# Modulation vectors of a diffusion block: TensorE matmuls with the weights as moving operand, in four column quarters, where VectorE made multiply-and-sum passes

## The chip, the core and the metric

The kernel runs on one core of a Trainium2 chip. The metric is device microseconds of one execution, as a median over runs. The core's engines are TensorE (PE, with its weight loads shown apart as PEld), VectorE (DVE), ScalarE (ACT) and GpSimd (POOL); SyncE (SP) issues the DMA transfers. Each engine works through its own instructions in program order and waits on semaphores for the others.

## What is computed

The program is a first block (a gated delta rule mixer and a convolutional GLU, both modulated) followed by a second block of two layers. Only the first one's modulation is touched:

```python
s_lat = jax.nn.silu(c)[:, None, :]            # [1, 1, 1024]
s_ctx = jax.nn.silu(c_ctx)[None, None, :]
mod_l = jnp.split(s_lat @ w_mod[i] + b_mod[i], 6, axis=-1)   # w_mod [1024, 6144]
mod_c = jnp.split(s_ctx @ w_mod[i] + b_mod[i], 6, axis=-1)
h_lat = modulate(rms_norm(x_lat, norm1_g[i]), mod_l[0], mod_l[1])
h_ctx = modulate(rms_norm(x_ctx, norm1_g[i]), mod_c[0], mod_c[1])
y_ctx, y_lat = gdn_mixer(h_ctx, h_lat, ...)
x_lat = x_lat + mod_l[2] * y_lat
h_lat = modulate(rms_norm(x_lat, norm2_g[i]), mod_l[3], mod_l[4])
x_lat = x_lat + mod_l[5] * conv_glu(h_lat, ...)
```

The sequence has 512 positions, the context 256, the model 1024 features. `mod_l` is a vector of 6144 values, and of `mod_c` only the first 2048 are used. The first 2048 of both are needed before anything can enter the mixer's projections; the other 4096 of `mod_l` only after the mixer.

## The kernel before

Features lie on partitions, positions on columns. A modulation vector is kept by feature: `modl` is [128, 48] (column j holds features 128j to 128j+127), `modc` is [128, 16]. Weights come from DRAM in blocks [128, 1024] (512 KB) through `wraw` (L136), a ring of three buffers. For most products ACT makes a rounded high part (L110), DVE or POOL the low part (L119), and TensorE takes three matmuls for each k tile (L157 to L159).

Stages of the first block, in the order of the program text:

- **mod**: `Modulation.__init__` makes silu of `c` and `c_ctx` by feature, and spreads both as rows over all partitions (`rowl`, `rowc`: 16 diagonal tiles on DVE, L1292, 16 matmuls with a matrix of ones, L1293, 4 copies on ACT, L1294). `by_tensor` makes columns 9 to 15 of both vectors: 7 blocks of w_mod stationary, two moving columns, 56 matmuls (L1316). `column(j, 1024)` makes columns 0 to 8: a load of 128 rows of w_mod's transpose, then for each of the two vectors one pass of DVE that multiplies by the silu row and sums (L1305), 18 passes.
- **h**: the norm of x and of the context (L247 to L256), and `modulated`: for each of 8 k tiles x * r (L1338, on POOL here), a high part on ACT (L1349), the modulated value (L1350) and the low part (L119) on DVE.
- **gat, prep0 to prep7**: the mixer's projections head by head, and small inverses (`inv`).
- **scan0 to scan3**: the recurrence by pairs of heads; scan 0, then scan 1, then 2 and 3 together. Lines L1653 to L1744.
- **fill**: work that the second block and the gates need, listed in `others` as units with a cost each: 8 gates (5.1), the norm of the memory (5), for each of two layers 8 blocks of keys (2.6) and 4 of values (5.1). Units are written into the program until their summed cost passes 32 ahead of the scans, and 4.6 more for each step of a scan. `mod.column(j, 512, ...)` for the other 32 columns of `modl` stands inside the gates, keys and values: two loads of 256 KB (`fill_C`) and two passes of DVE (L1305) each, 64 in all.
- **gout**: the mixer's output product, which needs all scans; `modl` is next used from there on.

The recorder that builds the program puts each engine's instructions into an order of its own, by dependencies, with the scans' steps at a higher priority than the fills; so the place of a fill is known from the built program.

Of the kernel before, what the change touches and what calls it, by code (L numbers as in the profile page):

```python
# [27 lines left out]
class Prog:  # L28
    """The program's pools and the parts that its stages share. Tiles of one tag are handed out in the order
    of the program, so what is to run ahead has a tag of its own."""  # L30
# [21 lines left out]
    def tiles(self, name, **kw):  # L52
        """a pool whose tiles wait for the users of their own bytes alone"""
        return self.tc.tile_pool(name=name, bufs=1, reuse_waits="tile", **kw)

    @contextmanager
    def pool(self, name, keep=False, **kw):
        """tiles of a stage; with keep, of several stages (tile(..., keep=True))"""
# [13 lines left out]
    def xt(self, dtype=F32R):  # L72
        """tiles of the products' operand, of all stages"""
# [6 lines left out]
    def banks(self, **bufs):  # L80
        """cuts PSUM's 8 banks in tags; within another, those that it leaves"""
# [24 lines left out]
    # exact split of a float32 value in two parts of 12 significant bits  # L106
# [14 lines left out]
    def split(self, src, tag, bufs, scale=None, n=512, le="v", keep=False, pool=None):  # L121
        """(hi, lo) of src, or of src * scale (scale: one value per partition)"""
# [38 lines left out]
    def gemm_block(self, ps, w, X, C, c0, kt, n=512, k0=0, first=True, last=True):  # L161
        """ps[128, n] += sum_k w[:, k, c0:c0+128]^T X[k]"""
# [7 lines left out]
    def strip(self, name, b, X, n=512):  # L170
        """block b of 128 output features: [128, n] in PSUM"""
# [4 lines left out]
    def rows_gemm(self, name, b0, X, pst):  # L176
        """products by position: pst[t] = X[:, tile t]^T w, 512 columns, in blocks of two k tiles"""
# [41 lines left out]
    def rsqrt(self, src, n, y, m, t, parts=1):  # L219
        """y = (src / n + EPS) ** -0.5, m = src / n + EPS; one Newton step on exp(-log(m) / 2); in parts of the  # L220
        columns where the next step waits for it"""
# [20 lines left out]
    def square_add(self, acc, x, last=False, scale=1.0):  # L242
        """acc + (scale * x) ** 2, per partition"""
# [9 lines left out]
    def rstd_rows(self, acc, n, width=512):  # L253
        """1 / rms by position, on all partitions"""
# [11 lines left out]
    def sigmoid(self, z, a):  # L266
        """a = 1 / (1 + exp(-z))"""
        nc = self.nc
        nc.vector.scalar_tensor_tensor(a, z, -1.0, z, ALU.mult, ALU.min)     # -|z|
        nc.scalar.activation(a, a, AF.Exp)  # L270
        nc.scalar.activation(a, a, AF.Ln, bias=self.one)
        nc.vector.scalar_tensor_tensor(a, z, 0.0, a, ALU.min, ALU.subtract)  # log of the sigmoid
# [4 lines left out]
def blocks(w, cols, C, kt=None):  # L277
    """[K, N] -> [nb, 128, kt * C]: block b holds columns cols[b*C:(b+1)*C], K split in kt tiles"""
# [28 lines left out]
def rope_tables():  # L307
    """cos, sin of 16 frequencies, 8 times; sin with the signs of the keys' products"""
# [1779 lines left out]
```

## Time and profile before

| | us |
|---|---|
| median of three runs (lowest to highest) | 3739.19 (3737.09 to 3744.71) |
| span of the profiled execution | 3736.5 |
| PE busy, share of the span | 3565.1, 95% |
| DVE busy, share of the span | 2461.0, 66% |
| ACT busy, share of the span | 1780.5, 48% |
| POOL busy, share of the span | 1273.6, 34% |

The profile is of one execution, on the kernel's one core. The table of windows shows the busy time of each engine in a stretch, the number of instructions in brackets, and the granted clock of TensorE as a share of 2.4 GHz (0.50 is the lower level, 1.2 GHz). Matmuls are pipelined: the record of one is longer than the distance to the next, so a busy PE can still be waiting inside its pipeline. "Idle before" is the time an engine stood still ahead of a group, with what ended it.

### The profile page before, as it was taken

How to read it: one execution, taken by the hardware profiler on the slowest of the kernel's cores; microseconds unless marked ns; L12 is line 12 of the kernel's file. 1: busy time of each engine (PE TensorE's matmuls, PEld its weight loads, DVE VectorE, ACT ScalarE, POOL GpSimd, SP SyncE). 2: the span in 40 equal slices, each digit the busy share in tenths (PEclk: the TensorE clock that was granted, in tenths of full speed). 3: DMA queues.
4: the chain of work that ended last, by engine and by line, in shares of the span. 5: the costliest groups of instructions: out<-in, count | busy, mean ns of one | idle time of the engine just before them, and what ended most of it. 6: DMA issues, size and time to landing. Idle time of an engine off the chain costs nothing. (4 is left out here: it accounts for less than half of the span.)

```text
span 3736.5 us, 51792 instructions
## 1 busy us (share of the span) xinstructions
PE 3565.1 (95%) x19280; PEld 2872.1 (77%) x19280; DVE 2461.0 (66%) x3770; ACT 1780.5 (48%) x3214; POOL 1273.6 (34%) x1173
## 2 busy tenths in 40 slices
PE   7998899899999998999999999999998999999998
PEld 5887788778888776687777888876676877778886
DVE  8887685655535788875556665369888755556643
ACT  3766454344434354565544443245456555444431
POOL 4476774322211555332121221125544311212212
PEclk7999899999999898999999999998899999999999
DMA  5346675433343111222243333421112322533332
GB/s 171 104 108 179 205 236 168 138 132 97 98 123 109 46 57 51 84 80 87 85 152 102 118 97 99 128 89 49 44 52 80 102 73 90 161 113 96 96 101 91
DMA packets 228955, 401.04 MB, mean 107 GB/s; under 512 B 77280, under 2 KB 118496, under 8 KB 228704
## 3 DMA queue, kind: packets, MB, share of 16 engines
q1 hardware_dynamic: 228704, 397.74, 34.7%
q8 instruction: 152, 2.49, 0.3%
q14 instruction: 99, 0.81, 0.1%
HBM read 347.58 MB, written 47.97 MB: 106 GB/s over the span
## 5 line engine op out<-in xcount | busy, mean ns | idle before, releaser
L159 PE MATMUL ffn_psg<-xo_X,ffn_wl 128*128 128x512 f32 x704 | 274.7, 390 | 0.0
L158 PE MATMUL ffn_psg<-xo_X,ffn_wh 128*128 128x512 f32 x704 | 273.9, 389 | 0.0
L157 PE MATMUL ffn_psg<-xo_X,ffn_wh 128*128 128x512 f32 x704 | 273.9, 389 | 0.0
L119 DVE TENSOR_TENSOR ffn_wl<-ffn_wr,ffn_wh 128x1024 fp32r<-128x1024 f32 x88 | 153.5, 1745 | 19.7 <-ACT ffn_wh L110 19.7
L719 DVE TENSOR_TENSOR ffn_z<-ffn_psg,xo_ry 128x512 f32<-128x512 f32 x88 | 60.7, 691 | 142.9 <-PE ffn_psg L159 142.6
L157 PEld LDWEIGHTS ffn_psg<-xo_X,ffn_wh 128*128 128x128 f32 x704 | 132.1, 188 | 27.9 <-issue 0.5
L159 PEld LDWEIGHTS ffn_psg<-xo_X,ffn_wl 128*128 128x128 f32 x704 | 132.1, 188 | 27.8 <-issue 0.5
L158 PEld LDWEIGHTS ffn_psg<-xo_X,ffn_wh 128*128 128x128 f32 x704 | 132.1, 188 | 27.6
L1210 POOL TENSOR_TENSOR ffn_z<-ffn_z,ffn_z 128x512 f32<-128x512 f32 x44 | 57.3, 1301 | 274.4 <-DVE ffn_z L719 233.9
L119 DVE TENSOR_TENSOR f_wl<-f_wr,f_wh 128x1024 fp32r<-128x1024 f32 (+1 forms) x48 | 56.8, 1183 | 129.3 <-ACT f_wh L110 129.3
L1142 POOL TENSOR_TENSOR br_acc<-br_acc,br_za 128x512 f32<-128x512 f32 x32 | 44.7, 1397 | 284.9 <-DVE br_za L1141 232.9
L158 PE MATMUL glu_psg<-gout_X,glu_wh 128*128 128x512 f32 x352 | 138.1, 393 | 3.0 <-DVE gout_X L1346 3.0
L159 PE MATMUL f_psg<-ffn_U,f_wl 128*128 128x512 f32 x352 | 140.8, 400 | 0.0
L157 PE MATMUL glu_psg<-gout_X,glu_wh 128*128 128x512 f32 x352 | 138.3, 394 | 2.1 <-ACT gout_X L1345 2.1
L158 PE MATMUL f_psg<-ffn_U,f_wh 128*128 128x512 f32 x352 | 138.7, 394 | 0.0
L157 PE MATMUL f_psg<-ffn_U,f_wh 128*128 128x512 f32 x352 | 138.0, 392 | 0.0
L159 PE MATMUL glu_psg<-gout_X,glu_wl 128*128 128x512 f32 x352 | 137.8, 392 | 0.0
L110 ACT ACTIVATE ffn_wh<-ffn_wr 128x1024 fp32r<-128x1024 f32 x88 | 93.6, 1064 | 92.2 <-PE ffn_psg L158 67.5
L1059 POOL TENSOR_TENSOR hg_hlv<-hg_hz,hg_hX 128x256 f32<-128x256 f32 x128 | 111.1, 891 | 75.8 <-issue 20.1
L110 ACT ACTIVATE f_wh<-f_wr 128x1024 fp32r<-128x1024 f32 (+1 forms) x48 | 47.5, 989 | 167.3 <-PE f_psg L158 139.8
L119 DVE TENSOR_TENSOR glu_wl<-glu_wr,glu_wh 128x1024 fp32r<-128x1024 f32 x44 | 56.4, 1282 | 102.6 <-ACT glu_wh L110 102.4
L119 POOL TENSOR_TENSOR hg_hB<-hg_hA,hg_hB 128x512 fp32r<-128x512 f32 x64 | 103.1, 1622 | 60.4 <-ACT hg_hB L110 53.0
(860 smaller groups left out, 11867.4 us busy)
## 6 DMA issues: line engine op xcount, KB each, us to landing
ffn_wr<-in_f_w_dram SPq DMA_DIRECT2D x88, 512.0 KB, 3.6
hg_wr<-in_w_in_dram SPq DMA_DIRECT2D x56, 512.0 KB, 3.5
br_wr<-in_w_in_dram SPq DMA_DIRECT2D x48, 512.0 KB, 3.6
glu_wr<-in_ffn_in_dram SPq DMA_DIRECT2D x44, 512.0 KB, 3.4
fill_C<-in_w_mod_dram SPq DMA_DIRECT2D x64, 256.0 KB, 4.7
f_wr<-in_f_w_dram SPq DMA_DIRECT2D x32, 512.0 KB, 3.6
prep_wr<-in_gdn_in_dram SPq DMA_DIRECT2D x24, 512.0 KB, 3.6
fill_wr<-in_x_wk_dram SPq DMA_DIRECT2D x16, 512.0 KB, 4.6
```

Of the source, the lines that this page charges most:

```text
L110: nc.scalar.activation(hi, src, AF.Copy)
L119: e.tensor_tensor(lo, src, f32(hi), ALU.subtract)
L157: nc.tensor.matmul(ps, wh, xh, start=start, stop=False)
L158: nc.tensor.matmul(ps, wh, xl, start=False, stop=False)
L159: nc.tensor.matmul(ps, wl, xh, start=False, stop=stop)
L719: p.nc.vector.tensor_tensor(t, ps, p.r, MULT)
L1059: e.tensor_tensor(dv, sv, xv.unsqueeze(3).broadcast_to([P, n, m, 16]), MULT)
L1142: nc.gpsimd.tensor_tensor(G.acc[m], G.acc[m], a, ADD)
L1210: nc.gpsimd.tensor_tensor(z1, z1, z3, MULT)
```

## The change

`w_mod` is now laid out in 12 blocks of 512 columns, each [128, 8 k tiles * 512], loaded as four pieces of 512 KB through the ring `wraw`. `Modulation.columns(b, new)` makes four columns of `modl` (and of `modc` for b under 4) from one block: 8 matmuls with the silu values as the stationary operand (32 columns for each k tile, of which two are not zero) and 512 columns of w_mod moving; k tile k writes the quarter of PSUM's partitions that begins at 32 * (k % 4). ACT copies the [128, 512] result, four matmuls with a [128, 2] selection matrix (a new constant, `sel`) sum the quarters and turn the rows into columns, and one or two additions on DVE put the bias on.

```diff
+    def columns(self, b, new):
+        p, nc = self.p, self.p.nc
+        ps = p.ps()
+        for h in range(2):
+            for i in range(2):
+                w = p.wraw(p.ins["w_mod"][b][:, (h * 2 + i) * 1024:(h * 2 + i + 1) * 1024])
+                for j in range(2):
+                    k = h * 4 + i * 2 + j
+                    q = slice(32 * (k % 4), 32 * (k % 4) + 32)
+                    nc.tensor.matmul(ps[q], self.sc[:, k], w[:, j * 512:j * 512 + 512], start=h == 0, stop=h == 1)
+        t = new()
+        nc.scalar.copy(t, ps)
+        ps = p.ps()
+        for j in range(4):
+            nc.tensor.matmul(ps[:, 2 * j:2 * j + 2], t[:, j * P:j * P + P], p.cconst("sel"), start=True, stop=True)
+        v = ps[:, :8].rearrange("p (j w) -> p j w", w=2)
+        c = slice(4 * b, 4 * b + 4)
+        for i, dst in enumerate((p.modl, p.modc) if b < 4 else (p.modl,)):
+            nc.vector.tensor_tensor(dst[:, c], v[:, :, i], p.col("b_mod")[:, c], ADD)
...
-        e = nc.vector if a is None and k % 2 == 0 else nc.gpsimd
+        e = nc.vector if k % 2 == 0 else nc.gpsimd
...
-        mod.column(16 + m, 512, pool, "C", 8)
-        mod.column(24 + l * 12 + m, 512, pool, "C", 8)
-        mod.column(32 + l * 12 + n, 512, pool, "C", 8)
+        if m % 2 == 1:
+            todo.append((2.5, lambda m=m: mod.columns(4 + m // 2, lambda: z("z2"))))
+            if l == 0 and i % 2 == 1:
+                todo.append((2.5, lambda i=i: mod.columns(8 + i // 2, lambda: z("z2"))))
...
-            mod.by_tensor()
-            for j in range(9):
-                mod.column(j, 1024)
+            for b in range(4):
+                mod.columns(b, lambda: p.t("md", 2))
```

`column`, `by_tensor` and the rows of silu are gone. Blocks 0 to 3 stand in stage mod. Blocks 4 to 11 are fill units of their own with a cost of 2.5 each, four after the gates 1, 3, 5 and 7 and four after the first layer's values. The budget of fills is as it was (32, then 4.6 a step), so 6 gates and 2 blocks are written ahead of the scans where 7 gates were, and the later units move back. In `modulated` half of the products x * r go to DVE, in stage h too. Lines after the class are 7 lower than before (L1895 was L1902).

On DVE, the end of stage mod and the beginning of stage h. Before, with the last passes of `column` (L1305; ISA rows with one column are reads of the accumulator), the scales (L1325), and the first modulated tile:

```order
L1305 ISA mod_wmj_314,modl<-mod_wm_312,rowl,vec 128x1024
L1305 ISA modl 128x1
L119 TENSOR_TENSOR prep_wl_676<-prep_wr_673,prep_wh_675 128x1024
L1305 ISA mod_wm_312,modc<-mod_wm_312,mod_rowc_102,vec 128x1024
L1305 ISA modc 128x1
L1325 SCALAR_TENSOR_TENSOR h_gs_86_385<-modl,vec 128x8
L1325 SCALAR_TENSOR_TENSOR h_gs_111_443<-modc,vec 128x8
L1350 TENSOR_SCALAR h_mh_387<-h_mh_387,h_gs_86_385,modl 128x512
L119 TENSOR_TENSOR h_X_390<-h_mh_387,h_X_389 128x512
```

and after, where L1312 adds the bias and L1331 is x * r:

```order
L119 TENSOR_TENSOR gat_wl_503<-gat_wr_500,gat_wh_502 128x1024
L1312 TENSOR_TENSOR modl<-mod_psg_239,vec 128x4
L1312 TENSOR_TENSOR modc<-mod_psg_239,vec 128x4
L1318 SCALAR_TENSOR_TENSOR h_gs_66_314<-modl,vec 128x8
L1318 SCALAR_TENSOR_TENSOR h_gs_91_372<-modc,vec 128x8
L119 TENSOR_TENSOR prep_wl_605<-prep_wr_602,prep_wh_604 128x1024
L1343 TENSOR_SCALAR h_mh_316<-h_mh_316,h_gs_66_314,modl 128x512
L119 TENSOR_TENSOR h_X_319<-h_mh_316,h_X_318 128x512
L1331 TENSOR_TENSOR h_mh_344<-mod_xl_126,h_ry_271 128x512
```

The passes are gone from this place, and the low part of the weights of the first head (prep_wl), whose load comes after the 16 pieces of w_mod and after gat_wr in the ring, now stands between the scales and the first modulated tile.

On PE, the beginning of stage mod after (mod_psg is the bank of a block, h_psa the sums of the two norms, gat_psg the first product of stage gat); x2 means two in a row. The first block, and the rows around the sum of the second norm:

```order
L1303 MATMUL mod_psg_142<-mod_wr_143,silc 32x512 x2
L256 MATMUL h_psa_269<-h_sq_266,ones 128x512
L1303 MATMUL mod_psg_142<-mod_wr_147,silc 32x512 x2
L1303 MATMUL mod_psg_142<-mod_wr_151,silc 32x512 x2
L1303 MATMUL mod_psg_142<-mod_wr_155,silc 32x512 x2
L1308 MATMUL mod_psg_161<-cstt,mod_md_159 128x2 x4
L1303 MATMUL mod_psg_168<-mod_wr_169,silc 32x512 x2
L256 MATMUL h_psa_303<-h_sq_300,ones 128x256
L1303 MATMUL mod_psg_168<-mod_wr_173,silc 32x512 x2
```

Behind them stand the rest of block 1, blocks 2 and 3, and then the first product (L157). The second norm's sum now stands between the first and the second piece of block 1.

On PE, a block among the steps of scan 0 after (scan_psc and scan_psd are the two directions, L1677 and L1695 the steps' matmuls):

```order
L1303 MATMUL fill_psg_5477<-fill_wr_5478,silc 32x512 x2
L1303 MATMUL fill_psg_5477<-fill_wr_5482,silc 32x512 x2
L1303 MATMUL fill_psg_5477<-fill_wr_5486,silc 32x512 x2
L1677 MATMUL scan_psc_5432<-scan_S_1032_5309,scan_wq_5263 64x128 x2
L1677 MATMUL scan_psd_5437<-scan_S_1034_5316,scan_wq_5281 64x128 x2
L1695 MATMUL scan_psc_5432<-scan_y_5431,scan_kd_5254 128x128 x2
L1695 MATMUL scan_psd_5437<-scan_y_5436,scan_kd_5272 128x128 x2
L1677 MATMUL scan_psc_5455<-scan_S_1064_5443,scan_wq_5263 64x128 x2
L1303 MATMUL fill_psg_5477<-fill_wr_5490,silc 32x512 x2
L1677 MATMUL scan_psd_5459<-scan_S_1066_5450,scan_wq_5281 64x128 x2
L1695 MATMUL scan_psc_5455<-scan_y_5431,scan_kd_5254 128x128 x2
L1308 MATMUL fill_psg_5496<-cstt,fill_z_1079_5494 128x2 x4
```

Before, nothing of the modulation stood on PE here. Steps of the scan stand between the third piece and the fourth, which waits for a buffer of the ring, and between the fourth and the selection.

On PE, the end of the scans. Before:

```order
L1724 MATMUL scan_psg_8560<-scan_y_8473,scan_sQK_8156 64x128 x3
L1724 MATMUL scan_psg_8582<-scan_y_8480,scan_sQK_8192 64x128 x3
L1724 MATMUL scan_psg_8604<-scan_y_8487,scan_sQK_8214 64x128 x4
L1902 MATMUL gout_psg_8639<-cstt,scan_O_7579 128x128
L1902 MATMUL gout_psg_8639<-cstt,scan_O_7941 128x128
```

and after:

```order
L1717 MATMUL scan_psg_8305<-scan_y_8203,scan_sQK_7861 64x128 x4
L1717 MATMUL scan_psg_8327<-scan_y_8210,scan_sQK_7883 64x128 x4
L157 MATMUL fill_psg_8350<-fill_X_7275,fill_wh_8353 128x256
L158 MATMUL fill_psg_8350<-fill_X_7276,fill_wh_8353 128x256
L159 MATMUL fill_psg_8350<-fill_X_7275,fill_wl_8354 128x256
```

Before, the steps of the scans are followed at once by the transposes of their results (gout_psg, L1902), and in the last 50 rows of the scans only sixteen transposes of two other heads stand among the steps. After, 96 matmuls of 256 columns and 16 transposes of the fills stand behind the last step, ahead of the same transposes, and fills stand among the last steps too. From gout on, PE's order is the same.

## Rows read from the trace of the kernel before

**Rows 1.** Windows: stretch, busy us of each engine, instructions in brackets, granted clock, DMA share, GB/s.

```profile
0.00:20.00 20.00, 10.99 (x50) 9.14 (x51) 12.47 (x40) 10.35 (x24) 8.25 (x11) 1.00 0.92 321
20.00:57.00 37.00, 21.95 (x99) 21.14 (x97) 33.54 (x53) 7.05 (x13) 14.65 (x10) 0.50 0.65 219
...
333.00:405.00 72.00, 61.10 (x409) 48.83 (x408) 51.69 (x82) 45.53 (x91) 48.27 (x57) 0.95 0.81 251
405.00:512.00 107.00, 97.01 (x784) 83.33 (x783) 84.97 (x189) 54.15 (x139) 65.98 (x86) 0.89 0.79 237
512.00:591.00 79.00, 75.13 (x726) 64.37 (x726) 56.66 (x124) 43.86 (x126) 58.64 (x80) 1.00 0.61 171
591.00:698.00 107.00, 107.00 (x871) 95.66 (x871) 60.94 (x128) 33.84 (x93) 46.68 (x70) 1.00 0.62 185
698.00:731.00 33.00, 23.62 (x164) 19.28 (x163) 31.13 (x98) 15.15 (x58) 15.21 (x22) 0.78 0.31 101
...
512.00:530.00 18.00, 16.05 (x122) 13.55 (x122) 17.84 (x38) 10.20 (x33) 17.61 (x18) 1.00 0.62 182
```

**Rows 2.** Groups by line, 0 to 57.3 us: busy us, mean ns; idle before, releaser.

```profile
L1305 DVE CUSTOM_DVE_ANT_0 mod_wmj<-mod_wm,rowl,vec 128x1024 f32<-128x1024 f32 x9 | 14.0, 1551 | 0.2 <-DMA mod_wm<-in_w_mod_dram 0.2
L1305 DVE CUSTOM_DVE_ANT_0 mod_wm<-mod_wm,mod_rowc,vec 128x1024 f32<-128x1024 f32 x9 | 12.8, 1422 | 0.0
...
L119 DVE TENSOR_TENSOR prep_wl<-prep_wr,prep_wh 128x1024 fp32r<-128x1024 f32 x1 | 1.2, 1215 | 0.0
...
L1294 ACT COPY rowl<-mod_psa 128x512 f32<-128x512 f32 x2 | 1.2, 585 | 3.3 <-PE mod_psa L1293 3.3
...
L110 ACT ACTIVATE prep_wh<-prep_wr 128x1024 fp32r<-128x1024 f32 x1 | 1.1, 1057 | 4.6 <-DMA prep_wr<-in_gdn_in_dram 4.6
```

**Rows 3.** Timeline, 27 to 60 us: start, us, engine, line, output and inputs, idle before.

```profile
28.94 1.22 PE L256 MATMUL h_psa<-h_sq,ones 128*128 128x256 f32 x2 [1.66 <-DVE h_sq L250]
...
57.24 0.55 DVE L1350 TENSOR_SCALAR h_mh<-h_mh,h_gs,modl 128x512 f32<-128x512 f32 x1 [0.82 <-ACT h_X L1349]
...
57.82 0.69 DVE L119 TENSOR_TENSOR h_X<-h_mh,h_X 128x512 fp32r<-128x512 f32 x1
...
59.00 1.66 DVE L119 TENSOR_TENSOR h_X<-h_mh,h_X 128x512 fp32r<-128x512 f32 x1
```

**Rows 4.** The tile mod_wr: ns min/median/max of its matmuls, and its loads.

```profile
L1316 PE MATMUL mod_pso<-mod_silc,mod_wr x112: 170/353/353, 17.1 to 43.3; 128*128 128x2 f32 x112
...
DMA to landing us min/median/max: 3.5/6.3/7.5
```

**Rows 5.** Timeline of PE, 403.4 to 403.9 and 734.2 to 734.5 us.

```profile
403.40 0.39 PE L158 MATMUL fill_psg<-h_X,fill_wh 128*128 128x512 f32 x1
403.71 0.32 PE L1684 MATMUL scan_psc<-scan_S,scan_wq 128*64 128x128 f32 x1
403.73 0.32 PE L1684 MATMUL scan_psd<-scan_S,scan_wq 128*64 128x128 f32 x1
403.87 0.27 PE L1684 MATMUL scan_psc<-scan_S,scan_wq 128*64 128x128 f32 x1
...
403.98 0.27 PE L1684 MATMUL scan_psc<-scan_S,scan_wq 128*64 128x128 f32 x1
...
734.22 0.39 PE L157 MATMUL gout_psg<-fill_X,gout_wh 128*128 128x512 f32 x1
734.44 0.39 PE L158 MATMUL gout_psg<-fill_X,gout_wh 128*128 128x512 f32 x1
```

**Rows 6.** The tile fill_C: the passes of DVE among the fills, ns min/median/max.

```profile
L1305 DVE CUSTOM_DVE_ANT_0 fill_C<-fill_C,rowl,vec x32: 734/752/1835, 338.5 to 524.1; 128x512 f32<-128x512 f32 x32
```

**Rows 7.** Timeline of DVE and of PE, 441 to 443 us.

```profile
441.98 0.41 DVE L1715 TENSOR_TENSOR scan_S<-scan_Sa,scan_psd 128x256 f32<-128x256 f32 x1
...
442.44 0.71 PE L1686 MATMUL scan_psd<-scan_S,scan_wq 128*128 128x128 f32 x4 [1.33 <-DVE scan_S L1715]
```

**Rows 8.** PE's waits, 698 to 735 us, the longest: us in total, times, longest.

```profile
PE gout_psg L1902 <- DVE scan_O L1744: 5.2, 1, 5.2
```

More of the change, by code (lines that the diff above doesn't have):

```diff
@@ L335, in constants @@
     k.add("ident", np.eye(128, dtype=np.float32))
+    k.add("sel", np.stack([(np.arange(128) % 32 == i).astype(np.float32) for i in range(2)], 1))
     return k
@@ L464, in first_arrays @@
     out = {}
-    out["w_mod"] = np.ascontiguousarray(g["w_mod"][0].T).reshape(48, 128, 1024)
-    out["w_mods"] = blocks(g["w_mod"][0], np.arange(1152, 2048), 128)
+    out["w_mod"] = blocks(g["w_mod"][0], np.arange(6144), 512)
     w = g["gdn_w_in"][0]
@@ L1276, with __init__ @@
 class Modulation:
-    def __init__(self, p, row):
+    def __init__(self, p, pool):
         nc = p.nc
-        self.p = p
-        rowc = p.t("rowc", 1, 1024)
-        self.rows = row, rowc
-        self.sc = sc = p.small([P, 8, 2], "silc", 1)
+        self.p, self.pool = p, pool
+        self.sc = sc = pool.tile([P, 8, 32], F32, tag="silc", name="silc")
+        nc.vector.memset(sc, 0.0)
         a = p.small([P, 16], "sila", 1)
-        for i, (n, row) in enumerate((("c", row), ("c_ctx", rowc))):
+        for i, n in enumerate(("c", "c_ctx")):
@@ L1287, in __init__ @@
             nc.vector.tensor_tensor(sc[:, :, i], p.col(n), p.sigmoid(p.col(n), a[:, 8 * i:8 * i + 8]), MULT)
-            for q in range(2):
-                ps = p.ps("ab"[i])
-                for j in range(4):
-                    dg = p.t("dg", 4, P)
-                    nc.vector.tensor_scalar(dg, p.ident, sc[:, q * 4 + j, i:i + 1], None, MULT)
-                    nc.tensor.matmul(ps[:, j * P:j * P + P], p.ones, dg, start=True, stop=True)
-                nc.scalar.copy(row[:, q * 512:q * 512 + 512], ps)
@@ L1295, in __init__ @@
         p.modl = p.cst.tile([P, 48], F32, tag="modl", name="modl")
         p.modc = p.cst.tile([P, 16], F32, tag="modc", name="modc")
-    def column(self, j, n, pool=None, tag="wm", bufs=4):
-        p = self.p
-        for o in range(0, 1024, n):
-            t = p.load(p.ins["w_mod"][j][:, o:o + n], tag, bufs, n, pool=pool)
-            for i, dst in enumerate((p.modl, p.modc) if j < 16 else (p.modl,)):
-                out = t if i == 1 or j >= 16 else p.t("wmj", 1, n)
-                p.nc.vector.tensor_tensor_reduce(out, t, self.rows[i][:, o:o + n], 1.0,
-                                                 (dst if o else p.col("b_mod"))[:, j:j + 1], MULT, ADD,
-                                                 accum_out=dst[:, j:j + 1])
@@ L1309, in by_tensor @@
-    def by_tensor(self):
-        p, nc = self.p, self.p.nc
-        ps = p.ps("o")
-        for j in range(7):
-            w = p.wraw(p.ins["w_mods"][j])
-            for k in range(8):
-                nc.tensor.matmul(ps[:, 2 * j:2 * j + 2], w[:, k * P:k * P + P], self.sc[:, k], start=k == 0, stop=k == 7)
-        v = ps[:, :14].rearrange("p (j w) -> p j w", w=2)
-        for i, dst in enumerate((p.modl, p.modc)):
-            nc.vector.tensor_tensor(dst[:, 9:16], v[:, :, i], p.col("b_mod")[:, 9:16], ADD)
+    def columns(self, b, new):
+        p, nc = self.p, self.p.nc
+        ps = p.ps()
[15 more added lines that the diff above has]
+            nc.vector.tensor_tensor(dst[:, c], v[:, :, i], p.col("b_mod")[:, c], ADD)
@@ L1842, in gdn @@
             p.stage = "mod"
-            mod = Modulation(p, ga.tile([P, 1024], F32, tag="rowl", name="rowl"))
+            mod = Modulation(p, ga)
             xl = [p.load(p.ins["xT"][k], "xl", 8) for k in range(8)]
```

## The prediction

> **What bounds the kernel now.** I read the table of windows first. Between 20 and 57 us DVE is busy for 33.54 of 37 us and PE for 21.95, at a granted clock of 0.50 [rows 1]: VectorE sets the end of stage mod. The groups by line say with what: the 18 passes of L1305 take 14.0 + 12.8 = 26.8 us, and they hardly wait for their loads (0.2 us) [rows 2]. The first modulated tile starts at 57.24 [rows 3]. That is one place for a gain.
>
> The second is the scans. Scan 0 runs in 405 to 512 us: 784 matmul instructions in 107 us, 7.33 a microsecond, with a PE idle for 10.0 us and a mean clock of 0.89. The next window, the end of scan 0 and scan 1 with the same kind of fills, has 726 in 79 us, 9.19 a microsecond, at full clock; the one after has a PE that never stands still [rows 1]. What differs is DVE: 84.97 of 107 us in the first, 56.66 of 79 in the second. Most of the 64 fill passes of L1305, 0.75 us each and at most 1.8, lie in the slow stretch [rows 6], and the steps of the scan queue behind them: scan_S of one direction gets DVE only at 441.98, right behind such passes, and PE waits 1.33 us for it [rows 7]. From 591 us on the passes are gone and PE is the bound. So the change takes work from an engine that is the bound in two stretches, and puts it on the one that is the bound everywhere else.
>
> **Stage mod.** DVE's 26.8 us go, PE's 112 instructions of by_tensor too. What comes next is the loads: still 8 MB, now 16 pieces through a ring of three. Two more things stand in line. The second norm's sum, which was at 28.94 [rows 3] behind a chain of squares on POOL that the change leaves alone, now stands inside block 1 on PE, so that 11 of the 16 pieces are worked on after 29 us. And prep_wl, two places behind the last piece in the ring, now precedes the first modulated tile.
>
> A piece takes 3.5 us from issue to landing at least, and 6.3 in the middle when many are queued [rows 4]. A matmul of the new kind has two instructions of 512 columns. In the scan a product with 128 float32 columns follows the one before at 0.16 and 0.11 us, and those of the two halves of the array start 0.02 us apart [rows 5]: the halves run at once. By 0.11 us a 512-column matmul takes 2 x 4 x 0.11 = 0.88 us at full clock, and if quarters run at once like halves, so does the pair of one piece. The selection has 8 instructions that are bound by their stationary operand like L1316's, 0.17 us at best and 0.35 at half clock [rows 4]: 1.4 or 2.8 us. The copy takes 0.59 [rows 2].
> At full clock the ring is the limit: four pieces take 4/3 x (3.5 + 0.88) = 5.8 us, 2.75 blocks 16 us, so the last piece is done by 45 and the one before, which gives prep's weights their buffer, shortly ahead of it. They then need 3.5 + 1.06 (cast) + 1.2 (low part) [rows 2, 4]: the first tile starts at some 51, a gain of 6. At half clock a block takes 4 x 1.76 + 0.6 + 2.8 = 10.4 us, 2.75 of them 28.7, and the tile comes at 59, a loss of 2. The clock was 0.50 while PE was busy for 22 of 37 us, 1.00 in the 20 us before [rows 1]; the new stretch has as many gaps, so I take the middle: **-2 (-6 to +2)**.
>
> **Stage h.** L119 takes 1.66 us beside a product on POOL and 0.69 without one [rows 3]. Half of the products move to DVE; four tiles are made while the scales are awaited, so two of 0.69 us come on DVE's path and two slow L119 go: 2 x 0.69 - 2 x 0.97 = -0.6. Together with the context's: **-1 (-3 to +1.4)**.
>
> **Ahead of the scans** (333 to 405) PE is idle for 10.9 us [rows 1]. Two blocks replace a gate there, and 20 us of DVE passes go, but chains on POOL go on: **-2 (-5 to +3)**.
>
> **Relief of the scans.** Upper end: the slow stretch at the rate of the next, 784 / 9.19 = 85.3 us, is a gain of 21.7, and 512 to 530, the last of the passes, with 122 in 18 us at that rate 4.7: 26. Lower end: of PE's idle time, 10.0 us + 1.95 in these two stretches, I give 8 to DVE, and to the clock nothing. The stretch beside it is the nearest row, since its scan and fills are the same; a little off it for additions and copies that are new: **-20 (-26 to -8)**.
>
> **New work on PE.** Six blocks come after the scans' start. Each has four pairs: 4 x 0.88 = 3.5 us if pairs run one after the other, 1.8 if pieces of different quarters overlap too; I take 2.6, plus 1.4 for the selection: 4.0 us, 24 in all. One gate of 24 matmuls moves behind the start, at 0.22 us each (their distance in the stream) [rows 5]: 5.3. Sum **+29.5 (+24 to +35)**. The Trainium skill (TensorE: Matmul & The Clock Gate, section Measured speedup vs the span model) gives 2.38 times for three column tiles of 32; at 0.79 a tile a pair would take 1.1 us, and by that estimate a block 3.3 + 1.4 at the middle of overlap, the sum 4 us higher.
>
> **Waits of a block.** The fourth piece needs the buffer that the first pair gives back, so it lands 3.5 us later. PE's queue behind it holds scan steps and the next unit's products, and DVE waits for the former. But five to seven rows of scan steps, some 2 us, stand ahead of that pair, as the order shows; similar rows stand ahead of the selection. I leave 0.5 us for each of six: **+3 (0 to +18)**, the upper end being the whole 3 us.
> The Trainium skill (TensorEngine Tiling (Array Packing), section Key Properties) speaks against such mixing: a change of the tiling mode drains TensorE. Here a product of halves starts 0.31 us behind a full 512-column one, whose like follows at 0.22 [rows 5]: 0.09 us lost. With some four changes a block that is 2 us in all, inside the range above; with the whole 0.39 us record of a matmul lost each time, by that rule at its worst, it would be 9.
>
> **The tail.** From 698 to 731 PE is idle for 9.4 us, and busy at a mean clock of 0.78 with short dependent products [rows 1]; 5.2 of it is the wait of gout for the last output of the scan [rows 8]. The order now has fills up to the last steps and 112 instructions behind them, 11 us or more by the distances above at full clock. The wait goes entirely; and half of the remaining 14 us or so that the steps leave unused (33 us with 164 instructions, which at 9.19 take 18): **-12 (-5 to -15)**. This is no new work: what lies here is missing from the saturated stretch before it.
>
> **Sum.** -2 - 1 - 2 - 20 + 29.5 + 3 - 12 = -4.5. On the span of 3736.5 that is 3732.0; the median of the runs is 2.7 above the profiled execution, so **3734.7**. A measurement of this kernel tells about 0.2% (7.5 us) from no change: below 3731.7 counts as faster, above 3746.7 as slower. The forecast lies in between, near the lower edge; the small terms give it a range of 3726 to 3745.
>
> **Rivals.**
> *Relief in full.* The scans reach the rate of the next window at once, and pieces overlap in four quarters: -26 in place of -20 and 6 x 1.8 + 8.4 + 5.3 = 24.5 in place of 29.5, with a start at full clock (-6): 3734.7 - 6 - 5 - 4 = 3719.7. For it: the neighbouring stretch does run so, and halves start 0.02 us apart. Against: the low clock around the start, and that the loads of one block come one after the other.
> *Quarters take turns.* If two matmuls into different quarters of one bank don't overlap, each pair costs 1.76 us: a block 7.0 + 1.4 instead of 4.0, 6 x 4.4 = 26 more, and some 5 in stage mod and ahead of the scans: 3766. It decides from a block of 6 us on: the 12 us that it takes to leave the band above, by six. Against it stand the halves; for it, that no row shows four quarters.
> *The ring starves PE.* Same result for another reason: a block takes four loads in the time in which a gate takes one, so the next unit's weights are late as well, by 3.5 us for the load and 2.3 for cast and low part. Six times 3 us in place of 0.5: 3750. Speaking for it, no more than three loads are ever under way; against, the steps in between.
> *The passes weren't what held the scans.* If the slow stretch owes its rate to POOL (65.98 of 107 us) or to the chains themselves, the relief is 8: 3747, at the edge of slower.
>
> **Chances.** Forecast 0.42, of which 0.13 ends below 3731.7 and 0.03 above 3746.7; relief in full 0.24; quarters in turn 0.13; starving ring 0.13; passes not the cause 0.08, half of it within. Faster 0.13 + 0.24 = 0.37; slower 0.03 + 0.13 + 0.13 + 0.04 = 0.33; the rest, 0.30, within 0.2%. The range of 8 in 10 leaves out one in ten at each side: part of the full relief, and the upper part of the quarters in turn: 3715 to 3764.
>
> **What would show it.** In the new profile: the first two matmuls of a pair start within some 0.05 us of each other and follow the previous pair at 0.9 us, not 1.8; the first modulated tile starts between 51 and 59 us, with the clock of 30 to 57 deciding where; the scan steps of DVE start where PE's product ends; scan 0 lasts some 85 to 95 us instead of 107; the waits of PE for L1303's loads sum to less than 5 us; no wait is left ahead of gout, and PE is busy up to it. The prediction is wrong if a pair takes 1.7 us at full clock, if PE waits for DMA in the blocks, or if scan 0 is as slow without the passes.

## The result and the profile after

The changed kernel takes 3780.12 us (median of 4 runs, 3775.29 to 3782.63) against 3740.28 for the kernel before on the same chip: a ratio of 1.0106, with an interval of 1.0092 to 1.0120. It is slower by 40 us; 3734.7 was forecast, with a range up to 3764. The profiled execution spans 3780.6 us, 44.1 more than before.

These are the windows of the changed kernel (stretch, busy us of each engine, instructions in brackets, granted clock, DMA share, GB/s), to be held against [rows 1]; the last one ends where gout begins.

```profile
20.00:57.00 37.00, 24.28 (x87) 8.50 (x87) 12.12 (x24) 8.26 (x14) 5.87 (x5) 0.67 0.65 217
...
333.00:405.00 72.00, 61.28 (x430) 45.80 (x429) 29.62 (x48) 38.32 (x77) 50.84 (x71) 0.86 0.69 214
405.00:512.00 107.00, 102.80 (x724) 80.67 (x723) 50.01 (x115) 56.96 (x149) 36.99 (x56) 0.83 0.55 161
512.00:600.00 88.00, 85.29 (x716) 69.74 (x715) 42.65 (x104) 41.74 (x120) 57.51 (x95) 0.99 0.57 169
600.00:700.00 100.00, 97.56 (x787) 80.52 (x783) 47.80 (x103) 32.13 (x92) 40.24 (x61) 0.95 0.66 202
...
700.00:771.00 71.00, 63.49 (x513) 56.03 (x511) 50.41 (x124) 26.89 (x78) 22.56 (x31) 0.97 0.56 179
```

DVE is relieved as meant: 50 us instead of 85 in 405 to 512, 12 instead of 33.5 in stage mod. But PE executes fewer instructions in 405 to 512 than before (724 against 784), and its clock is lower in the two windows that hold the first blocks: 0.86 and 0.83 against 0.95 and 0.89. The fills begin at 335.5 us (333.3 before) and gout at 771.1 (727.7): of the 44.1 us, 41.2 are lost between these two places.

The scans' own steps fall behind late. These are the last steps on DVE of scan 0, of scan 1, and of scans 2 and 3 in the changed kernel; in the kernel before they start at 507.69, 588.31 and 717.48:

```profile
505.46 0.42 DVE L1708 TENSOR_TENSOR scan_S<-scan_Sa,scan_psd 128x256 f32<-128x256 f32 x1 [2.81 <-PE scan_psd L1695]
...
592.27 0.42 DVE L1708 TENSOR_TENSOR scan_S<-scan_Sa,scan_psd 128x256 f32<-128x256 f32 x1 [0.76 <-PE scan_psd L1695]
...
741.61 0.42 DVE L1708 TENSOR_TENSOR scan_S<-scan_Sa,scan_psi 128x256 f32<-128x256 f32 x1 [0.28 <-PE scan_psi L1695]
```

Stage mod, single PE instructions (start, us, engine, line, output and inputs, count, idle before):

```profile
18.85 1.08 PE L1303 MATMUL mod_psg<-mod_wr,silc 128*32 128x512 f32 x8
...
49.52 1.92 PE L1303 MATMUL mod_psg<-mod_wr,silc 128*32 128x512 f32 x4 [2.18 <-DMA mod_wr<-in_w_mod_dram]
...
56.47 0.79 PE L157 MATMUL gat_psg<-h_X,gat_wh 128*128 128x512 f32 x1 [2.42 <-ACT h_X L1342]
```

The quarters overlap: two pieces, eight instructions of 512 columns, take 1.08 us at the upper clock. The last piece comes at 49.5, at the lower clock, and the first product at 56.47 instead of 57.26. Counted in products done (L157 to L159), PE is 1.2 us ahead of the kernel before at 80 us and 3.8 ahead at 231; at 260 it is 2 us behind. It lost this between 230 and 260 us, where this execution has a granted clock of 0.83 and the one before 1.00 (the window of the changed kernel, then of the kernel before):

```profile
230.00:260.00 30.00, 28.26 (x329) 22.82 (x328) 20.56 (x39) 22.71 (x47) 11.56 (x19) 0.83 0.39 97
```

```profile
230.00:260.00 30.00, 29.38 (x364) 24.39 (x364) 20.92 (x40) 24.67 (x49) 14.31 (x21) 1.00 0.43 101
```

Now a block among the fills. First PE around the second one, then SP's queue at the same time, then what SP waited for in 374 to 381 us (total, times, longest), with the instruction of POOL that ended this wait:

```profile
376.18 0.39 PE L159 MATMUL fill_psg<-h_X,fill_wl 128*128 128x512 f32 x1
376.50 1.91 PE L1303 MATMUL fill_psg<-fill_wr,silc 128*32 128x512 f32 x12
384.67 1.92 PE L1303 MATMUL fill_psg<-fill_wr,silc 128*32 128x512 f32 x4 [6.26 <-DMA fill_wr<-in_w_mod_dram]
387.33 1.87 PE L1308 MATMUL fill_psg<-cstt,fill_z 128*128 128x2 f32 x8 [0.74 <-ACT fill_z L1305]
389.41 0.79 PE L157 MATMUL fill_psg<-h_X,fill_wh 128*128 128x512 f32 x1 [0.21 <-ACT fill_wh L110]
```

```profile
374.75 5.72 SPq L98 DMA_DIRECT2D scan_k<-h_dk  x2
380.56 0.38 SPq L136 DMA_DIRECT2D fill_wr<-in_w_mod_dram  x1
```

```profile
SPq L98 <- POOL scan_kd L1647: 4.0, 1, 4.0
...
379.51 0.61 POOL L1647 TENSOR_TENSOR scan_kd<-scan_k,gtkd 128x256 f32<-128x256 f32 x1
```

Here three pieces need 1.9 us of PE. The fourth needs the buffer that the first gave back soon after 376.5; but its load was issued only at 380.56, because SP issues in order and stood before a load of the scan (scan_k) whose own buffer POOL still read. So PE stood for 6.26 us, and what came next ran at the lower clock: 0.57 in the window 384 to 396, and the 512-column products of the next gate follow each other at 0.43 us until 394 instead of 0.23. This is the longest of seven such waits; the other six are 0.6 to 2.4 us.

What PE waited for between 333 and 780 us (total, times, longest), the three largest:

```profile
PE fill_psg L1303 <- DMA fill_wr<-in_w_mod_dram: 14.7, 7, 6.3
PE gout_psg L1895 <- DVE fill_z L1896: 4.1, 1, 4.1
PE fill_psg L1308 <- ACT fill_z L1305: 3.2, 2, 2.5
```

The wait of gout for the scan [rows 8] is gone, and a wait for the fills that now stand behind the scans has taken its place.

### The profile page after: what moved, and what is told of

Its sections match the earlier page's. It is cut to its first block, busy times and chain, and to the rows that moved or that the text cites. A ratio compares the mean times of both kernels' runs of the same rounds, so it can differ in the third digit from the quotient of the medians.

```text
span 3780.6 us, 51842 instructions
## 1 busy us (share of the span) xinstructions
PE 3616.3 (96%) x19424; PEld 2880.6 (76%) x19424; DVE 2365.4 (63%) x3613; ACT 1785.6 (47%) x3222; POOL 1230.7 (33%) x1165
## 5 line engine op out<-in xcount | busy, mean ns | idle before, releaser
L159 PE MATMUL ffn_psg<-xo_X,ffn_wl 128*128 128x512 f32 x704 | 274.7, 390 | 0.0
L157 PE MATMUL ffn_psg<-xo_X,ffn_wh 128*128 128x512 f32 x704 | 273.9, 389 | 0.0
L159 PEld LDWEIGHTS ffn_psg<-xo_X,ffn_wl 128*128 128x128 f32 x704 | 132.2, 188 | 28.0 <-issue 0.5
L157 PEld LDWEIGHTS ffn_psg<-xo_X,ffn_wh 128*128 128x128 f32 x704 | 132.2, 188 | 27.5 <-issue 0.5
L1211 POOL TENSOR_TENSOR ffn_z<-ffn_z,ffn_z 128x512 f32<-128x512 f32 x44 | 57.3, 1302 | 274.4 <-DVE ffn_z L720 233.8
L159 PE MATMUL f_psg<-ffn_U,f_wl 128*128 128x512 f32 x352 | 140.8, 400 | 0.0
L157 PE MATMUL glu_psg<-gout_X,glu_wh 128*128 128x512 f32 x352 | 138.2, 393 | 2.1 <-ACT gout_X L1338 2.1
L157 PE MATMUL f_psg<-ffn_U,f_wh 128*128 128x512 f32 x352 | 138.0, 392 | 0.0
L159 PE MATMUL glu_psg<-gout_X,glu_wl 128*128 128x512 f32 x352 | 137.9, 392 | 0.0
L110 ACT ACTIVATE br_wh<-br_wr 128x1024 fp32r<-128x1024 f32 x96 | 81.0, 843 | 83.7 <-PE br_psg L158 63.7
```

The lines of the kernel that those rows point to most:

```text
L110: nc.scalar.activation(hi, src, AF.Copy)
L157: nc.tensor.matmul(ps, wh, xh, start=start, stop=False)
L159: nc.tensor.matmul(ps, wl, xh, start=False, stop=stop)
L1211: nc.gpsimd.tensor_tensor(z1, z1, z3, MULT)
```

## The experiments

The theory after the result: the loss is the blocks among the fills, and most of it the ring of three buffers that they share with the weights. The rivals: the blocks' own work on PE; the new start or the products moved from POOL; and, as a part of the theory, that the low clock behind the waits weighs more than the waits.

The experiments ran in groups on five chips, each with the kernel before beside it (medians of 3736.0 to 3742.7 us); the ratios and intervals are against that. Where times of two groups are subtracted, the difference by the ratios, in us of 3740, stands behind it; it is known to some 6 to 9 us.

**Which part of the change.** Four kernels. In the first, the kernel before without the passes among the fills (a copy of the bias takes the place of the 32 columns):

```diff
-        mod.column(16 + m, 512, pool, "C", 8)
-        mod.column(24 + l * 12 + m, 512, pool, "C", 8)
-        mod.column(32 + l * 12 + n, 512, pool, "C", 8)
+            nc.vector.tensor_copy(p.modl[:, 16:48], p.col("b_mod")[:, 16:48])
```

> The kernel before, with the 64 passes of VectorE among the fills and their 64 loads left out (columns 16 to 47 of modl are set to the bias alone). Theory A, that the passes held the scans (as predicted): the scans gain 20 to 26 us, the time is 3715 to 3720. Theory B, that TensorE had enough other work while the scan's steps queued behind the passes, so that they cost little: 3730 to 3736.

Measured: 3738.43 us, 0.9982 of the kernel before on the same chip (0.9964 to 0.9999). At the end theory B holds (2 us above its range). On the way theory A does, in the profiled execution, which is 9 us faster than the median: these are single DVE instructions, the last step of scan 1 before and without the passes, then the last of scans 2 and 3 before and without.

```profile
588.31 0.42 DVE L1715 TENSOR_TENSOR scan_S<-scan_Sa,scan_psd 128x256 f32<-128x256 f32 x1
```

```profile
565.92 0.41 DVE L1715 TENSOR_TENSOR scan_S<-scan_Sa,scan_psd 128x256 f32<-128x256 f32 x1
```

```profile
717.48 0.41 DVE L1715 TENSOR_TENSOR scan_S<-scan_Sa,scan_psi 128x256 f32<-128x256 f32 x1
```

```profile
715.06 0.42 DVE L1715 TENSOR_TENSOR scan_S<-scan_Sa,scan_psi 128x256 f32<-128x256 f32 x1
```

22.4 us are gained by the end of scan 1 and 2.4 are left at the end of scans 2 and 3. Part of what is lost is a stretch at the lower clock between 568 and 586 us (granted clock 0.50 with PE busy throughout, so 9 us); the rest was not taken apart.

The second leaves the eight blocks out of the changed kernel in the same way:

```diff
-        if m % 2 == 1:
-            todo.append((2.5, lambda m=m: mod.columns(4 + m // 2, lambda: z("z2"))))
...
-            if l == 0 and i % 2 == 1:
-                todo.append((2.5, lambda i=i: mod.columns(8 + i // 2, lambda: z("z2"))))
```

> The changed kernel, with the eight blocks among the fills left out (columns 16 to 47 of modl are set to the bias alone); the start is the new one. If the loss comes from the blocks among the fills alone, the time is that of the kernel before without its passes, to within 5 us, and 45 us or more under the changed kernel. If the new start or the products moved from GpSimd lose a part, it is over 5 us slower than the kernel before without passes.

Measured: 3728.13 us, 0.9958 (0.9941 to 0.9975). So the blocks cost 52 us (55), and new start and moved products lose nothing: this is 10 us under the first one's median, where at most 5 either way were expected, with intervals that overlap. In its profiled execution (7 us faster than the median) scan 1 ends as in the first one (565.47), but scans 2 and 3 end at 704.66, so that 12.8 of the 22.8 us are left there.

The third and the fourth put the halves of the change together with the other kernel's half:

```diff
             for b in range(4):
                 mod.columns(b, lambda: p.t("md", 2))
+            mod.make_rows(ga.tile([P, 1024], F32, tag="rowl", name="rowl"))
...
+        mod.column(16 + m, 512, pool, "C", 8)
```

> Blocks 0 to 3 at the start by TensorE as in the changed kernel, the other 32 columns by passes of VectorE among the fills as before (with the row of silu that they need). Theory: the start alone is worth nothing that lasts (its gain of some 3 us is lost again by 260 us): 3736 to 3744. Rival, the start as I priced it: 3733 to 3738. If the start were to blame for the loss: over 3750.

Measured: 3740.24 us, 0.9998 (0.9980 to 1.0016): nothing.

```diff
             mod.by_tensor()
             for j in range(9):
                 mod.column(j, 1024)
...
+            todo.append((2.5, lambda m=m: mod.columns(4 + m // 2, lambda: z("z2"))))
...
+                todo.append((2.5, lambda i=i: mod.columns(8 + i // 2, lambda: z("z2"))))
```

> Stage mod as before, the eight blocks among the fills by TensorE as in the changed kernel. Theory: the loss is all here, 3775 to 3785. Rival, that half of the loss comes from the new start or from the products moved to VectorE: 3755 to 3765.

Measured: 3778.05 us, 1.0094 (1.0066 to 1.0123): all of the loss. A variant of the third makes the row of silu as the first fill unit:

```diff
+    todo.append((0, lambda: mod.make_rows(mod.rowl, lambda: z("z2"))))
     for m in range(8):
```

> The new start without the passes of VectorE, as in the run with the new start and the old fills, but the row of silu on all partitions that the fills' passes need is made as the first fill unit, and not within the start. Theory: the start is then as in the changed kernel, the fills as before: 3728 to 3737. Rival, that the start's gain doesn't last to the end: 3738 to 3742.

Measured: 3745.56 us, 1.0014 (0.9999 to 1.0028), above both ranges. Later rows don't help; the start's gain doesn't reach the end beside the old fills.

**What of a block costs.** First the ring: the pieces of the eight blocks come through the ring C of eight buffers, a k tile (256 KB) each.

```diff
-                w = p.wraw(p.ins["w_mod"][b][:, (h * 2 + i) * 1024:(h * 2 + i + 1) * 1024])
...
+                        m = piece()
+                        nc.sync.dma_start(m, p.ins["w_mod"][b][:, k * 512:k * 512 + 512])
...
+            todo.append((2.5, lambda m=m: mod.columns(4 + m // 2, lambda: z("z2"), newc)))
```

> The changed kernel, but the pieces of the eight blocks among the fills come as sixteen... eight tiles of 256 KB through the ring of eight small buffers that the passes' loads used before, and no longer through the three buffers that the weights share. Theory W, that a good part of the 50 us is TensorE's waiting for pieces (14.7 us in the trace of the changed kernel) and the low clock behind the waits: 3755 to 3765. Theory P, that the blocks' own matmuls are the price whatever the loads do: 3772 to 3780.

Measured: 3744.86 us, 1.0015 (1.0004 to 1.0025): 35 us (34) less than the changed kernel, more than theory W had. The edit changes three things at once: whom the pieces share buffers with, how many buffers they have, and the size of a load. More buffers in the shared ring, or the pieces' loads in another engine's queue, were not tried. Its windows:

```profile
333.00:405.00 72.00, 64.25 (x500) 50.06 (x498) 35.44 (x55) 45.74 (x100) 50.60 (x67) 0.93 0.78 240
405.00:512.00 107.00, 107.00 (x837) 86.32 (x836) 52.67 (x123) 58.56 (x163) 58.26 (x97) 0.94 0.66 191
512.00:600.00 88.00, 87.20 (x821) 70.61 (x819) 48.89 (x111) 41.84 (x126) 51.39 (x82) 1.00 0.67 207
600.00:700.00 100.00, 99.70 (x798) 86.47 (x797) 66.87 (x140) 33.66 (x84) 42.83 (x61) 1.00 0.61 189
700.00:732.00 32.00, 25.37 (x213) 23.01 (x212) 22.96 (x65) 14.73 (x43) 5.40 (x8) 0.95 0.52 165
```

No wait of PE for a piece is left (one of 6.7 us for a block's copy is). The two sets of windows can be added up, from 333 us to the start of gout: PE's idle time (length less busy) is 10.7 + 4.2 + 2.7 + 2.4 + 7.5 = 27.6 us in the changed kernel and 7.8 + 0 + 0.8 + 0.3 + 6.6 = 15.5 here, 12 less. What the clock took, as length times what its share lacks to 1, is 10.1 + 18.2 + 0.9 + 5.0 + 2.1 = 36.3 and 5.0 + 6.4 + 0 + 0 + 1.6 = 13.1, 23 less. Together 35 us, of the 38.8 by which the stretch from the first fill to gout became shorter (435.6 to 396.8). By this count two thirds of the ring's price are the low clock. Not all of it stands behind the waits: taking 22 us from the first matmul of each block on, the clock's part is 22.2 in the changed kernel and 5.9 here, 16 of the 23 us. The rest comes from a stretch that holds no block and in which PE is never idle, with scan steps, small inverses, sums of the memory's norm and products of the fills. Its clock's part is 11.8 us in the changed kernel and 5.9 in the like stretch here (447.5 to 497). In the changed kernel:

```profile
467.00:526.00 59.00, 59.00 (x419) 49.60 (x418) 29.84 (x84) 26.92 (x91) 21.65 (x37) 0.80 0.34 98
```

Then the two halves of a block. Without loads, all matmuls read a resident tile:

```diff
-                w = p.wraw(p.ins["w_mod"][b][:, (h * 2 + i) * 1024:(h * 2 + i + 1) * 1024])
+                w = fixed if fixed is not None else p.wraw(p.ins["w_mod"][b][:, (h * 2 + i) * 1024:(h * 2 + i + 1) * 1024])
```

> The changed kernel, but the matmuls of the eight blocks among the fills read a tile that is in the chip already (their 32 loads are left out, the 32 columns come out wrong). What is left is the blocks' work on TensorE, with copies and selections. Theory P: work of 8 x 3.8 us on an engine that is the bound: 3755 to 3762, 27 to 34 us above the kernel without blocks (3728). Theory W: 3735 to 3745.

Measured: 3740.02 us, 0.9995 (0.9981 to 1.0010): the work on PE is 12 us (14) above the kernel without blocks, much less than theory P had, inside what theory W had.

With the loads through the shared ring and nearly no work:

```diff
+                    nc.tensor.matmul(ps[q, :8], self.sc[:, k], w[:, j * 512:j * 512 + 8], start=h == 0, stop=h == 1)
```

> The changed kernel, but the matmuls of the eight blocks among the fills take 8 moving columns in place of 512, and copy and selection are left out (the 32 columns come out wrong); all 32 loads and the waits for them stay. Theory W: 3745 to 3755, since the ring holds up TensorE and the next unit's weights with or without the work. Theory P: 3728 to 3738.

Measured: 3759.43 us, 1.0058 (1.0043 to 1.0073): 31 us (37) above the kernel without blocks, more than theory W had. PE's longest sum of waits in it, from 333 to 780 us:

```profile
PE fill_psg L1302 <- DMA fill_wr<-in_w_mod_dram: 20.1, 6, 6.9
```

So of 52 us the work is 12, loading that much in a ring of its own 5 (3744.86 less 3740.02; 7 by the ratios), and the loads through the three shared buffers, in place of eight of their own, 35.

**The quarters.** From the kernel with a ring of its own, all eight matmuls of a block into one quarter:

```diff
-                    q = slice(32 * (k % 4), 32 * (k % 4) + 32)
+                    q = slice(0, 32) if piece else slice(32 * (k % 4), 32 * (k % 4) + 32)
```

> The kernel with the pieces in a ring of their own, but the eight matmuls of each block among the fills all go into the first quarter of PSUM's partitions, one after the other, and the selection sums over 32 partitions. If quarters run at once, as the trace of the changed kernel has it (four instructions start within 0.03 us), this costs 8 x (6.8 - 2.2) = 37 us more than with quarters: 3775 to 3785. If the quarters bring nothing, or TensorE has that much room: 3745 to 3755.

Measured: 3803.21 us, 1.0168 (1.0146 to 1.0190), 18 us above the higher range. The first block of the two kernels, with one quarter and with four:

```profile
350.72 7.05 PE L1308 MATMUL fill_psg<-fill_C,silc 128*32 128x512 f32 x16
```

```profile
350.52 1.92 PE L1308 MATMUL fill_psg<-fill_C,silc 128*32 128x512 f32 x16
```

7.05 against 1.92 us: with all pieces there, four quarters run 3.7 times as fast. Eight blocks make 41 us of that; measured are 58 (57). The granted clock is lower as well (0.84 in 405 to 512 against 0.94); what else is in the rest was not taken apart.

**Waits or clock.** Eight useless matmuls into each block's accumulation, of a stationary operand of zeros, first where PE waits for the fourth piece, then ahead of the first piece:

```diff
+                if b >= 4 and h == 1 and i == 1:
+                    self.idle(ps, 8)
```

> The changed kernel, with eight useless matmuls (a stationary operand of zeros, a resident tile moving, 3.4 us at full clock) into the same accumulation of each block among the fills, between its third and its fourth piece, where TensorE waits for the fourth. Theory C, that more than half of the ring's price is the low clock that follows the waits: the filler keeps the clock up and the time is 3765 to 3778, below the changed kernel (3780) in spite of 8 x 3.4 = 27 us more work. Theory D, that the waits themselves and the late weights behind them are the price: the filler takes the place of waiting at first and of work then, 3780 to 3795.

```diff
+                if b >= 4 and h == 0 and i == 0:
+                    self.idle(ps, 8, True)
```

> The same eight useless matmuls ahead of the first piece of each block, where TensorE doesn't wait. Here they are added work under both theories: 27 us, less what the low clock makes dearer or an earlier landing of the first pieces saves: 3795 to 3812. If this is no slower than the run with the filler in the wait, the place of the filler doesn't matter and the clock behind the waits isn't the cause.

Measured: 3798.78 us (1.0166, 1.0149 to 1.0183) with the filler in the wait, 3780.94 (1.0118, 1.0103 to 1.0134) with it ahead. Both expectations missed, the wrong way round: the one is 4 us above theory D's range, the other 14 below its own. The windows with most blocks, in the wait and ahead:

```profile
405.00:512.00 107.00, 105.73 (x757) 79.31 (x755) 50.29 (x115) 55.29 (x141) 35.42 (x53) 0.88 0.56 160
...
600.00:700.00 100.00, 99.88 (x791) 75.34 (x788) 38.19 (x85) 28.69 (x87) 36.18 (x54) 0.91 0.56 170
```

```profile
405.00:512.00 107.00, 105.89 (x785) 82.08 (x784) 50.14 (x113) 59.27 (x155) 32.53 (x52) 0.90 0.55 160
...
600.00:700.00 100.00, 98.72 (x861) 79.19 (x860) 44.15 (x95) 31.94 (x94) 42.73 (x62) 1.00 0.61 190
```

By the same sums over the five windows, the filler in the wait takes the place of idle time (17.5 us, 10 less than in the changed kernel), and the clock's part stays at 37.5. The filler is 8 x 3.4 = 27 us of work; 27 less 10 is near the 18.7 (22) that it costs. But the clock's part has moved. In 22 us from the first matmul of each block on it is 10.3 instead of 22.2, and 6.8 of that is the second block's, where PE still waits 5.4 us behind the filler. The third and the seventh block, in the changed kernel and then with the filler in the wait:

```profile
409.00:431.00 22.00, 19.89 (x118) 14.03 (x119) 7.67 (x15) 13.87 (x32) 9.85 (x16) 0.92 0.84 252
614.00:636.00 22.00, 19.64 (x112) 14.28 (x112) 7.20 (x15) 5.10 (x14) 8.89 (x15) 0.77 0.66 205
```

```profile
409.00:431.00 22.00, 22.00 (x141) 15.23 (x141) 7.69 (x15) 14.49 (x34) 9.68 (x15) 1.00 0.82 250
632.00:654.00 22.00, 21.97 (x157) 14.31 (x156) 8.55 (x18) 6.47 (x20) 13.46 (x20) 1.00 0.65 195
```

Elsewhere it is 12 us more than in the changed kernel, in stretches without a block and without idle time:

```profile
466.50:530.00 63.50, 63.50 (x435) 52.49 (x438) 31.26 (x84) 28.25 (x93) 21.85 (x38) 0.76 0.34 96
...
591.50:632.00 40.50, 40.50 (x393) 33.86 (x393) 14.71 (x39) 14.26 (x55) 12.54 (x19) 0.79 0.49 145
```

So the time refutes theory C as it was put, that the filler pays for itself; that low clock follows the waits is not refuted, since it goes from the places where the filler ends the wait. Why it comes back elsewhere was not found.

Ahead of the first piece the same 27 us cost 0.8 (4.5, not clear of noise): idle time falls by 8.5 us and the clock's part to 24.0, 12 less, and the waits for pieces are 6.1 us in sum, in place of 14.7. In these two runs and in the one with a ring of its own fewer or shorter waits for pieces go with less low clock behind the blocks; no run holds the clock and leaves the waits, so the clock's share of the ring's price remains a count. The expectation took a filler ahead that is no slower than one in the wait to mean that the place doesn't matter and the clock isn't the cause. But the place matters, by 18 us, so nothing follows for the clock from that.

**Looking for a faster one.** From the kernel with its own ring (3744.86): the copy on DVE, and a cost of 0.5 for a block.

```diff
-        nc.scalar.copy(t, ps)
+        (nc.vector.tensor_copy if piece else nc.scalar.copy)(t, ps)
...
-            todo.append((2.5, lambda m=m: mod.columns(4 + m // 2, lambda: z("z2"), newc)))
+            todo.append((0.5, lambda m=m: mod.columns(4 + m // 2, lambda: z("z2"), newc)))
```

> The kernel with the pieces in a ring of their own, with the copy of a block on VectorE in place of ScalarE (TensorE waited 6.7 us for one copy that stood behind a wait of ScalarE's queue) and a cost of 0.5 in place of 2.5 for each block, so that fewer fills are left behind the scans (TensorE waits 7 us for their results there). If these waits are on the path: 3732 to 3739. If other work takes their place: 3742 to 3746.

Measured: 3768.47 us, 1.0077 (1.0053 to 1.0102), 22 us above the higher range. PE now waits 13.7 us for copies, four times, since DVE's queue stands still as well, and the cheaper blocks let more units in ahead of the scans: the first step of scan 0 comes at 419.0 us instead of 401.7. The two edits were not separated.

All blocks ahead of the gates, besides:

```diff
+    for b in range(4, 12):
+        todo.append((0, lambda b=b: mod.columns(b, lambda: z("z2"), newc)))
     for m in range(8):
```

> As the run before, with all eight blocks as the first fills, ahead of the gates, where TensorE stands still for 7 of 43 us (290 to 333) and 11 of 72 us (333 to 405) in the kernel before. If the blocks find that room: 3728 to 3736. If they delay the chains on GpSimd and ScalarE that the scans wait for, or wait for their 16 MB: 3745 to 3755.

Measured: 3799.51 us, 1.0160 (1.0138 to 1.0181), 45 us above the higher range. The idle time ahead of the scans is no room: DMA is busy to 0.91 there, PE's clock is 0.76, and scan 0 starts its steps at 469.7.

```profile
333.00:405.00 72.00, 59.06 (x384) 25.41 (x383) 18.18 (x44) 20.75 (x43) 42.58 (x76) 0.76 0.91 289
```

The other direction, the copy on ACT again, fewer fills ahead of the scans:

```diff
-GS, MORE, RB, F0, F1 = [[0], [1], [2, 3]], 2, 8, 32, 4.6
+GS, MORE, RB, F0, F1 = [[0], [1], [2, 3]], 2, 8, 25, 5.3
```

> The kernel with the pieces in a ring of their own and the copy on ScalarE, with a budget of 25 in place of 32 ahead of the scans (4 gates and 2 blocks instead of 6 and 2) and of 5.3 in place of 4.6 a step, so that as much is done by the end of the scans. The run with a lower cost for the blocks had seven gates and more blocks ahead and its first step of the scan came 17 us later (419 against 402 us). If what stands ahead of the scans is on the path and the fills behind them too: 3728 to 3738. If the scans only become slower by what they now hold: 3742 to 3750.

Measured: 3752.54 us, 1.0023 (1.0007 to 1.0039), above both ranges: no gain. No version with all its columns was faster than the kernel before; without loads the blocks' work alone brings it level (3740).

## Why the prediction was wrong

- **The step that failed is "Waits of a block", +3 us (0 to +18).** It measured 35 us: 3780.12 with the shared ring, 3744.86 with a ring of its own. The waits themselves are 14.7 us, where less than 5 was the sign given; that is still inside the term's range, the price is not. Three things were left out. Only six blocks were given a wait, but 7.3 of the 14.7 us stand in the two blocks ahead of the scans. The 3.5 us from issue to landing were counted from the moment the buffer came free; but SP's queue stands between, and in the longest wait the load of the fourth piece sat behind a load of the scan (issued at 380.56). And each wait was priced as time alone: by the count of the windows the low clock makes 23 of the 35 us, 16 of them in the 22 us from the beginning of a block on. The rival that the ring starves PE had the mechanism and a chance of 0.13, but the same price without the clock: 15 us.
- **The gains did not add up, a second failure of nearly the same size.** Stages mod and h, the stretch ahead of the scans, the relief and the tail made -37 in the sum; without blocks the kernel is 12 us faster than before. With +32 for the waits, +25 for this and -12 for the work, which was priced too high (17 us with its loads instead of 29.5), the 45 us between forecast and time are accounted for.
- **Relief of the scans, -20.** Right in size and place: 22.4 us by the end of scan 1 when the passes are simply left out. But it doesn't last: 2.4 and 12.8 at the end of the scans in the first and second experiment, and 2 and 12 us in the time. I had put the gain in a stretch into the sum without asking what is late next in scans 2 and 3. In the changed kernel itself scan 0's steps end 2 us earlier than before, scan 1's 4 later and the last ones 24 later.
- **New work on PE, +29.5 with a gate of 5.3.** Too large: 12 us without the loads, 17 with them. Four quarters do run at once (1.92 us for a block of sixteen instructions, where 0.88 for each pair would be 3.5), and part of the work finds room. The rival that quarters take turns is refuted; with eight blocks in one quarter its price was 58 us, where it had 31 (26 for six blocks and 5).
- **Stage mod, -2.** Right: 0.8 us at the first product, 1.2 at 80 us, and nothing in the end (0.9998 with the new start alone). The granted clock of 0.67 in 20 to 57 us is a mean, as I had split it: 0.98 until 33 us, 0.50 from there to 52.
- **The tail, -12.** At most half right. The wait of gout for the scan went, but gout waits for the last fills now (4.1 us instead of 5.2), and there are 29.5 us between the last step of the scans and gout instead of 10.2. The sum also counted the wait twice: its 5.2 us are among the 15 that the steps leave unused. By idle time and the clock's part together, what PE leaves unused from 700 us to gout is 9.6 us, against 15.3 before: some 6 gained by this count, which no run sets apart. The window of the kernel before:

```profile
700.00:728.00 28.00, 18.62 (x133) 14.40 (x132) 26.64 (x90) 12.64 (x53) 13.21 (x19) 0.79 0.31 101
```

- The Trainium skill's figure of 2.38 times for three quarters (TensorE: Matmul & The Clock Gate, section Measured speedup vs the span model) agrees in kind; here four gave 3.7. The Trainium skill's rule that a change of tiling mode drains TensorE (TensorEngine Tiling (Array Packing), section Key Properties) is not where the loss lies: without loads, but with all changes of mode, the blocks cost 12 us in all.

## What to carry to other kernels

A ring of buffers that feeds weights at one rate is a resource of its own: a unit that takes four buffers in two microseconds empties it here (three pieces used in 1.9 us, the fourth up to 6.3 us late), and everything behind it in the order waits too, so look who shares the ring and what stands ahead of the load in the issuing queue before counting matmuls. Price a wait of TensorE with the clock that follows it: here, by the count, more than the waits themselves. And ask of the relief that a stretch shows whether the next stretch can pass it on: of 22 us, 2 to 13 were left at the end of the scans.

## What the runs showed of the hardware

- Eight float32 matmuls of a 128 x 32 stationary operand and 512 moving columns take 1.92 us in four quarters of PSUM's partitions and 7.05 in one, both at the upper clock.
- Matmuls with a stationary operand of zeros in two quarters, put into waits, kept the granted clock at 1.00 behind two blocks (409 to 431 us, 632 to 654) where the kernel without them had 0.92 and 0.77. From 333 us to gout the clock took as much as without them (37.5 us against 36.3).
- A granted clock below 1.00 needs no idle time in PE's rows: 0.80 in 467 to 526 us of the changed kernel and 0.50 in 568 to 586 of the kernel without passes, with PE busy throughout.
- A load whose buffer is free still waits its turn in the queue of the engine that issues it: issued at 380.56 us behind a load that stood in the queue from 374.75 on, for a buffer that POOL read until 380.1.
